# A layer kernel whose second token half is also given transposed: norms spread on chip, rows no longer turned, fold stores on ACT's queue

## The chip, the cores and the metric

The kernel runs on one core of one Trainium2 chip. The metric is the device time of one execution in microseconds; the time before is the median of three runs. A profiled execution was recorded besides; its page and its trace are quoted in the text. Engines are named as the profile names them: PE (TensorE matmul), PEld (its weight load), DVE (VectorE), ACT (ScalarE), POOL (GpSimd), SP (SyncE, which here issues most DMAs).

## What is computed

One layer of a streaming encoder on 2048 tokens of width 1024, all in fp32. It has three sub-layers, each between two RMS norms:

```python
u = rms_norm(h, g_mix_pre); z = u @ w_in          # 1024 -> 2816 columns
qa, ka, va, qh, fh, ih, gh = jnp.split(z, IN_SPLITS, axis=-1)
ya = swa_with_sinks(qa, ka, va, sinks)            # sliding-window attention
yh = hgrn2(qh, fh, ih, gh, lb, onorm)             # gated linear recurrence, log of fh
h = h + rms_norm(concat(ya, yh) @ w_out, g_mix_post)
h = h + rms_norm(cross_attention(rms_norm(h, g_x_pre), rms_norm(mem, g_mem), wq, wk, wv, wo), g_x_post)
h = h + rms_norm(swiglu(rms_norm(h, g_ffn_pre)), g_ffn_post)
```

The change touches the first norm and the first projection, `u @ w_in`, and one stage that prepares the cross-attention.

## The kernel before

**Matmuls.** Every fp32 operand is kept as two parts of a lower precision, hi and lo (`split`, `split2`: hi is a copy made on ACT or POOL, lo is the difference made on DVE), and a product is three matmuls: hi hi, hi lo, lo hi (`mm3`, and `products` at lines 1032 to 1034). Most large products are done in blocks of 2 x 2 by seven products in place of eight (`seven`; kind `"o"` here), the first two blocks of the first projection by eight (`eight`, kinds `"q"` and `"p"`). A step is one of these products: 12 matmuls of 128x128 by 128x512.

**First half of the first projection** (`in_first`, `in_block`). The tokens are cut in two halves of 1024. For the first half, rows of x are loaded, normed (`normed`: Square with a row sum on ACT, two small operations on POOL for the reciprocal root, a scaling on DVE), turned by TensorE (line 449) and kept in four tiles, `raw`. Eleven blocks of 256 columns of `w_in` then run in the order of `ORDER`. `phases` drives them: at each step it traces the step's matmuls, then the operands of the step two ahead (`upto(g + 2)`), then one piece of what a former block left to do (`after`), then pieces of the resident operands `T`. Within a step, line 1047 copies a bank of PSUM away on ACT (`part`), and `out` puts results into a `pair` tile.

**What runs beside.** While the blocks run, the eight rows tiles of the second token half are prepared: `stream` loads one into a `pair` tile (lines 542 to 545; `beside` says which block takes which), `after` norms it (572 and 573) and, some steps later, turns it with eight transposes on TensorE and two ACT copies (`transposed`, lines 1284 and 1285) and stores it to `un_d` in device memory (587). At the end `fetch` loads `un_d` back in four tiles of 1 MB (489), and lines 519 to 527 split these into the hi and lo parts `u` with which the second half is projected.

**Gate columns.** Four of the blocks (columns 1280 to 1791, `C_FH`) hold the forget gate. For these `after` runs `decays`: the logarithm (637, ACT, with a table load before and after), a scan on DVE, a shift on POOL and three exponentials on ACT, one piece a step.

**Later stages.** The second half is projected (`in_proj`, `in_cols`) beside attention (`swa`) and recurrence (`hgrn`). `fold_cross` multiplies the cross-attention's weights with the memory: it stores eight row tiles to `qk_d` (321) and eight to `vo_d` (347), at the end of that stage with nothing beside it. Then the remaining blocks run, again through `phases`; their left operands are streamed from `y_d`, which attention and recurrence wrote.

**Order.** The kernel names engines, tiles and buffers (a pool tag has a fixed number of buffers, `bufs`). The framework makes each engine's queue from that when the program is built (line 1662): an instruction may be placed ahead of others that were traced before it when its operands and its buffer are ready earlier. `behind` ties the instructions in it to come after the last ACT and DVE instruction traced up to `mark`. Each engine works off its queue in order; a DMA that waits on SP's queue holds up the DMAs behind it. All DMAs but those with accumulation are issued by SP (`load`, `store`).

Of the kernel before, what the change touches and what calls it, by code (L numbers as in the profile page):

```python
# [11 lines left out]
F32 = mybir.dt.float32  # L12
# [6 lines left out]
P = 128  # L19
# [29 lines left out]
class Layer:  # L49
# [27 lines left out]
    def store(self, dst, src):  # L77
        self.nc.sync.dma_start(dst, src)
# [13 lines left out]

    def rstd(self, parts, n, role):
# [9 lines left out]
        r = self.small(role + "_r")  # L103
        nc.gpsimd.tensor_tensor(r, v, self.mhalf[:, 0:1], ALU.pow)
        return r
# [62 lines left out]
    def run(self):  # L168
# [4 lines left out]
        self.y_d = tc.dram_tile([NT, P, KT, P], F32, name="y_d")  # L173
        self.un_d = tc.dram_tile([KT, P, TB], F32, name="un_d")
        self.h1t_d = tc.dram_tile([NT, P, KT, P], F32, name="h1t_d")
# [101 lines left out]
    def fold_cross(self):  # L277
# [31 lines left out]
        for d in range(KT):  # L309
            th, tl = self.wcols(self.I["wq_x"], d, "A")  # L310
            o = self.io_tile("x")
            for q in range(2):
# [7 lines left out]
                if q:  # L320
                    self.store(self.qk_d[d * P:(d + 1) * P, :], o)
                yield
        for vT in projected(self.I["wv_x"]):
            yield
        for h in range(4):
# [17 lines left out]
            for mt in range(2):  # L343
                o = self.io_tile("x")
                for q in range(2):
                    nc.scalar.activation(o[:, q * 512:(q + 1) * 512], banks[mt][q], AF.Copy)
                self.store(self.vo_d[(2 * h + mt) * P:(2 * h + mt + 1) * P, :], o)
            yield
# [73 lines left out]
    def in_first(self):  # L422
# [60 lines left out]
        second = {}  # L483

        def fetch():
            for s in range(2):
# [11 lines left out]
        phases = self.phases([(lambda i, j, a, n: raw[i, j][:, a:a + n, :], 4, blocks, None, {})], T)  # L498
        next(phases)
# [14 lines left out]
        for _ in phases:  # L514
            pass
        for _ in get:
            pass
        u = []
        for s in range(2):
            u.append([])  # L520
            for q in range(2):
                self._n += 1
                t = self.big.tile([P, 2, 4, 512], F32R, tag="big", name=f"u1_{q}{s}")
                r = second[q, s]
                for k in (0, 2):
                    self.split2(r[:, k:k + 2], t[:, 0, k:k + 2], t[:, 1, k:k + 2], "A")
                u[s] += [(t[:, 0, k, :], t[:, 1, k, :]) for k in range(4)]
        return u

    def in_block(self, ca, cb, beside, get, between):  # L530
# [405 lines left out]
    def combined(self, get, nk, dst):  # L936
# [3 lines left out]
        for a, b in halves:  # L940
            def put(key, t, o, op):
                with self.behind():
# [3 lines left out]
            for x, y, key in (((0, 1), (0, 0), 5), ((1, 1), (0, 1), 7), (None, (0, 0), 6), (None, (1, 0), 4)):  # L946
# [5 lines left out]
                if key == 4:  # L952
                    put(4, o, t, ALU.subtract)
                else:
                    put(key, t, o, ALU.add if key == 6 else ALU.subtract)
                yield
# [709 lines left out]
```

## Time and profile before

| | |
|---|---|
| median of 3 runs | 2603.19 us (2600.45 to 2605.1) |
| the profiled execution | 2603.6 us |
| its span, from first to last instruction | 2601.7 us |
| mean granted clock of TensorE | 0.992 |
| first projection, first half | from the start to about 263 us |
| fold | ends at about 791 us |

A row of the profile's groups reads: line, engine, operation, tile written <- tiles read, shape, count | busy us, mean ns of one | idle us of the engine just before them, and what ended most of it. A row of a timeline has the start, the duration, the engine, the line, and in brackets the idle time before it with what ended that. A row of waits has the total, the times and the longest. The chain of waits is followed back from the last instruction to what released each.

### The profile page before, as it was taken

To read this page: it belongs to the slowest core of one execution; us is meant where nothing else is said; L and a number is where in the kernel's file an instruction comes from. 1 tells how busy PE (TensorE), PEld (TensorE's weight loads), DVE (VectorE), ACT (ScalarE), POOL (GpSimd) and SP (SyncE) were. 2 spreads that over 40 slices of the span, in tenths; PEclk is the share of its full clock that TensorE was granted. 3 is DMA by queue.
4 is the path that set the end of the run, shared out by engine and by line. 5 is a ranking of instruction groups with operands and counts; after the bars stand their busy time and mean duration, and the time that the engine had idled before them with its cause. 6 is when DMAs were issued, how large, how long until landed. Compare 5 with 4: busy or idle time off the path is not lost.

```text
span 2601.7 us, 34516 instructions
## 1 busy us (share of the span) xinstructions
PE 2528.0 (97%) x12160; PEld 2115.2 (81%) x12160; DVE 1746.0 (67%) x2773; ACT 1262.0 (49%) x2641; POOL 466.6 (18%) x651
## 2 busy tenths in 40 slices
PE   7989999999998999999999999999999999999998
PEld 6878788878997778888778888888888888888786
DVE  7675578887646568786785555576666656664756
ACT  5463366655654565565563333354333335443543
POOL 4240343320312224223320000000000000000022
PEclk9999999999999999999999999999999999999999
DMA  5434655484875998656984532353456434576798
GB/s 186 143 120 167 208 157 171 131 267 157 279 259 207 289 328 258 221 191 187 302 273 138 167 124 73 105 186 116 167 182 230 147 108 168 174 225 174 232 228 208
DMA packets 286350, 497.88 MB, mean 191 GB/s; under 512 B 20576, under 2 KB 143456, under 8 KB 286176
## 3 DMA queue, kind: packets, MB, share of 16 engines
q1 hardware_dynamic: 275520, 456.87, 52.3%
q0 software_dynamic: 10656, 38.80, 8.0%
q8 instruction: 96, 1.57, 0.2%
q14 instruction: 78, 0.64, 0.1%
HBM read 328.87 MB, written 166.72 MB: 190 GB/s over the span
## 4 chain that ended last, share of the span: by engine, by line
PE 80%; DMA 8%; DVE 4%; issue 3%; POOL 2%; ACT 2%; SPq 0%; DVEq 0%; POOLq 0%; ACTq 0%
PE psm L1032 22%; PE psm L1034 22%; PE psm L1033 22%; PE psg L163 2%; PE psg L164 2%; PE psg L165 2%; DMA row<-in_x_dram 1%; PE pss L1284 1%; DMA row<-h_d 1%; DMA u_d<-row 1%; DMA h_d<-row 1%; DMA x<-in_w_out_dram 1%; ACT junk L1369 1%; DMA pair<-in_x_dram 1%; DMA extra<-qk_d 0%
## 5 line engine op out<-in xcount | busy, mean ns | idle before, releaser
L1032 PE MATMUL psm<-T,S 128*128 128x512 f32 x2664 | 1036.4, 393 | 24.6 <-ACT S L896 13.8
L1033 PE MATMUL psm<-T,S 128*128 128x512 f32 x2664 | 1041.9, 391 | 0.0
L1034 PE MATMUL psm<-T,S 128*128 128x512 f32 x2664 | 1037.3, 392 | 2.6 <-DVE S L899 2.5
L1032 PEld LDWEIGHTS psm<-T,S 128*128 128x128 f32 x2664 | 503.3, 189 | 132.6 <-ACT S L896 15.1
L1034 PEld LDWEIGHTS psm<-T,S 128*128 128x128 f32 x2664 | 502.5, 189 | 109.2 <-DVE S L899 4.8
L1033 PEld LDWEIGHTS psm<-T,S 128*128 128x128 f32 x2664 | 503.2, 189 | 103.3
L896 ACT ACTIVATE S<-sum 128x512 fp32r<-128x512 f32 (+1 forms) x338 | 208.0, 619 | 340.1 <-PE psm L1034 331.7
L899 DVE TENSOR_TENSOR S<-sraw,S 128x512 fp32r<-128x512 f32 (+1 forms) x311 | 214.4, 697 | 224.4 <-ACT S L896 214.9
L899 DVE TENSOR_TENSOR S<-sum,S 128x512 fp32r<-128x512 f32 (+1 forms) x404 | 277.1, 690 | 84.3 <-ACT S L896 66.6
L1047 ACT ACTIVATE part<-psm 128x512 f32<-128x512 f32 x297 | 175.1, 592 | 174.9 <-PE psm L1034 168.0
L896 ACT ACTIVATE S<-sraw 128x512 fp32r<-128x512 f32 (+1 forms) x272 | 166.8, 617 | 154.7 <-PE psm L1034 143.1
L1398 POOL DMA_DIRECT2D row<-y_d x28 | 25.0, 892 | 1131.4 <-DMA sraw<-hid_d 964.8
L1369 ACT ACTIVATE junk<-row 128x512 f32<-128x512 f32 x160 | 99.7, 624 | 121.8 <-DVE row L1391 33.4
L899 DVE TENSOR_TENSOR T<-row,T 128x1024 fp32r<-128x1024 f32 x104 | 123.0, 1190 | 28.7 <-ACT T L896 28.5
L163 PE MATMUL psg<-u,whi 128*128 128x512 f32 x352 | 141.2, 401 | 1.0 <-POOL whi L145 1.0
L165 PE MATMUL psg<-u,wlo 128*128 128x512 f32 x352 | 139.5, 396 | 1.5 <-DVE wlo L146 1.5
L164 PE MATMUL psg<-u,whi 128*128 128x512 f32 x352 | 139.6, 397 | 0.0
L896 ACT ACTIVATE T<-row 128x1024 fp32r<-128x1024 f32 x104 | 105.8, 1027 | 23.7 <-DMA row<-in_w_down_dram 10.9
L146 DVE TENSOR_TENSOR wlo<-raw,whi 128x1024 fp32r<-128x1024 f32 x54 | 68.8, 1275 | 33.2 <-ACT whi L143 26.6
L898 POOL TENSOR_SCALAR S<-sum 128x512 fp32r<-128x512 f32 x66 | 49.0, 742 | 234.7 <-PE psm L1034 141.0
L1550 DVE TENSOR_TENSOR part<-psm,part 128x512 f32<-128x512 f32 x66 | 45.4, 688 | 64.6 <-PE psm L1034 64.5
L1541 DVE TENSOR_TENSOR row<-psm,part 128x512 f32<-128x512 f32 x66 | 45.5, 689 | 57.4 <-PE psm L1034 57.3
(329 smaller groups left out, 3644.3 us busy)
## 6 DMA issues: line engine op xcount, KB each, us to landing
sraw<-in_w_gate_dram SPq DMA_DIRECT2D x44, 512.0 KB, 4.9
sraw<-in_w_up_dram SPq DMA_DIRECT2D x44, 512.0 KB, 4.8
hid_d<-row SPq DMA_DIRECT2D x44, 512.0 KB, 2.7
h_d<-row SPq DMA_DIRECT2D x32, 512.0 KB, 6.9
y_d<-row SPq DMA_DIRECT2D x32, 512.0 KB, 3.6
sraw<-hid_d SPq DMA_DIRECT2D x32, 512.0 KB, 5.2
row<-h_d POOLq DMA_DIRECT2D x30, 512.0 KB, 8.1
row<-y_d POOLq DMA_DIRECT2D x28, 512.0 KB, 7.3
```

The lines of the kernel that those rows point to most:

```text
L146: nc.vector.tensor_tensor(lo, raw, f32(hi), ALU.subtract)
L163: nc.tensor.matmul(ps, ah, bh, start=(i == 0), stop=False)
L164: nc.tensor.matmul(ps, ah, bl, start=False, stop=False)
L165: nc.tensor.matmul(ps, al, bh, start=False, stop=(i == n - 1))
L896: self.nc.scalar.activation(hi, raw, AF.Copy)
L898: self.nc.gpsimd.tensor_scalar(hi, raw, 1.0, 1.0, ALU.mult, ALU.mult)
L899: self.nc.vector.tensor_tensor(lo, raw, f32(hi), ALU.subtract)
L1032: nc.tensor.matmul(ps, s[:, 0, k, :], t[:, 0, k, :], start=st, stop=False, **kw)
L1033: nc.tensor.matmul(ps, s[:, 0, k, :], t[:, 1, k, :], start=False, stop=False, **kw)
L1034: nc.tensor.matmul(ps, s[:, 1, k, :], t[:, 0, k, :], start=False, stop=sp, **kw)
L1047: nc.scalar.activation(t, ps, AF.Copy)
L1369: self.nc.scalar.activation(junk, a, AF.Square, scale=float(D) ** -0.5, accum_out=to)
```

## The change

Five things, which belong together except for the last.

- The host also hands over the second token half of x transposed, as `x_t` in four tiles of 128 x 4 x 512, and the gain `g_mix_pre` with a column per 128 features, `g_mix_t`. `fetch` loads these instead of `un_d`, two tiles a block from the blocks after the seventh on; `un_d`, the transposes and the stores are gone.
- The rows of the second half are still loaded, but only for their sums of squares: into a tag `xr` with one buffer, Square in place, and the reciprocal root goes into a column of `r_u`. One row tile belongs to each of the blocks 1 to 8. `pair` has six buffers instead of five.
- Beside the last block (`{10: [scaled]}`), `scaled` spreads the eight columns of `r_u` along the partitions with eight transposes into two banks, and multiplies the loaded tiles by gain and norms, four DVE operations of 128 x 512 a step, in four steps. `parted` then splits as before.
- `decays` yields once more before the logarithm.
- The stores to `qk_d` and `vo_d` are issued from ACT's queue (`put`) instead of SP's.

```diff
+    def put(self, dst, src):
+        self.nc.scalar.dma_start(dst, src)
...
-                    self.store(self.qk_d[d * P:(d + 1) * P, :], o)
+                    self.put(self.qk_d[d * P:(d + 1) * P, :], o)
...
-                self.store(self.vo_d[(2 * h + mt) * P:(2 * h + mt + 1) * P, :], o)
+                self.put(self.vo_d[(2 * h + mt) * P:(2 * h + mt + 1) * P, :], o)
...
-        return self.st_pool.tile([P, 2, D], F32, tag="pair", name=f"pair_{self._n}", bufs=5)
+        return self.st_pool.tile([P, 2, D], F32, tag="pair", name=f"pair_{self._n}", bufs=6)
...
-                    self.load(r, self.un_d[4 * q:4 * q + 4, :, s * 512:(s + 1) * 512].rearrange("k p t -> p k t"))
+                    self.load(r, I["x_t"][2 * s + q])
...
+        def scaled():
+            banks = []
+            for s in range(2):
+                ps = self.bank("sh"[s])
+                for i in range(4):
+                    n = 4 * s + i
+                    nc.tensor.transpose(ps[:, i * P:(i + 1) * P], self.r_u[:, n:n + 1].broadcast_to([P, P]), self.ident)
+                banks.append(ps)
+            for s in range(2):
+                for q in range(2):
+                    r = second[q, s]
+                    for k in range(4):
+                        with self.behind():
+                            nc.vector.scalar_tensor_tensor(r[:, k, :], r[:, k, :], g_t[:, 4 * q + k:4 * q + k + 1],
+                                                           banks[s], ALU.mult, ALU.mult)
+                    yield
...
-        beside = [(), (0,), (1, 2), (3,), (4,), (5,), (6,), (7,), (), (), ()]
+        beside = [(), (0,), (1,), (2,), (3,), (4,), (5,), (6,), (7,), (), ()]
...
-                  + self.in_block(*p, beside[i], get if i > 9 else (), None if i else lambda: x_loads(0, (2, 3)))
+                  + self.in_block(*p, beside[i], get if i > 7 else (), None if i else lambda: x_loads(0, (2, 3)))
...
-            for n in beside:
-                t = self.pair_tile()
-                self.load(t[:, 0, :], self.I["x"][TB + n * P:TB + (n + 1) * P, :])
-                x.append((n, t))
-            for _ in range(3):
+            for _ in range(2):
                 next(iter(get), None)
...
         def after():
-            for n, p in x:
-                self.normed(p[:, 0, :], p[:, 1, :])
+            for n in beside:
+                self._n += 1
+                t = self.st_pool.tile([P, D], F32, tag="xr", name=f"xr_{self._n}", bufs=1)
+                self.load(t, self.I["x"][TB + n * P:TB + (n + 1) * P, :])
+                x.append((n, t))
...
-            for _ in range(1 if C_FH <= c0 < C_IH else 4):
+            for _ in range(1 if C_FH <= c0 < C_IH else 3):
                 yield
-            for n, p in x:
-                self.store_transposed(self.un_d, n, self.transposed(p[:, 0, :], p[:, 1, :]))
+            for n, t in x:
+                ss = self.small("n_s")
+                nc.scalar.activation(t, t, AF.Square, accum_out=ss)
+                self.rstd([ss], D, "n", self.r_u[:, n:n + 1])
                 yield
...
         NCB = TB // 64
+        yield
         nc.scalar.activation(e1, f, AF.Ln)
```

More of the change, by code (lines that the diff above doesn't have):

```diff
@@ L91, in gain, with rstd @@
         return g
-    def rstd(self, parts, n, role):
+    def rstd(self, parts, n, role, r=None):
         nc = self.nc
@@ L102, in rstd @@
             nc.gpsimd.tensor_scalar(v, parts[0], 1.0 / n, EPS, ALU.mult, ALU.add)
-        r = self.small(role + "_r")
+        if r is None:
+            r = self.small(role + "_r")
         nc.gpsimd.tensor_tensor(r, v, self.mhalf[:, 0:1], ALU.pow)
@@ L173, in run @@
         self.y_d = tc.dram_tile([NT, P, KT, P], F32, name="y_d")
-        self.un_d = tc.dram_tile([KT, P, TB], F32, name="un_d")
         self.h1t_d = tc.dram_tile([NT, P, KT, P], F32, name="h1t_d")
@@ L483, in in_first @@
         second = {}
+        self.r_u = self.mc.tile([P, NPB], F32, name="r_u")
+        g_t = self.mc.tile([P, KT], F32, name="g_t")
+        u = [[], []]
         def fetch():
+            self.load(g_t, I["g_mix_t"])
             for s in range(2):
@@ L488, in fetch, with parted @@
                     r = self.pair_tile().rearrange("p a d -> p (a d)").rearrange("p (k t) -> p k t", k=4)
-                    self.load(r, self.un_d[4 * q:4 * q + 4, :, s * 512:(s + 1) * 512].rearrange("k p t -> p k t"))
+                    self.load(r, I["x_t"][2 * s + q])
                     second[q, s] = r
                     yield
-        beside = [(), (0,), (1, 2), (3,), (4,), (5,), (6,), (7,), (), (), ()]
+        def scaled():
[14 more added lines that the diff above has]
+                    yield
+        def parted():
+            for s in range(2):
+                for q in range(2):
+                    self._n += 1
+                    t = self.big.tile([P, 2, 4, 512], F32R, tag="big", name=f"u1_{q}{s}")
+                    for k in (0, 2):
+                        self.split2(second[q, s][:, k:k + 2], t[:, 0, k:k + 2], t[:, 1, k:k + 2], "A")
+                    u[s] += [(t[:, 0, k, :], t[:, 1, k, :]) for k in range(4)]
+        beside = [(), (0,), (1,), (2,), (3,), (4,), (5,), (6,), (7,), (), ()]
         get = fetch()
         blocks = [("q" if i == 0 else "p" if i < 2 else "o",)
-                  + self.in_block(*p, beside[i], get if i > 9 else (), None if i else lambda: x_loads(0, (2, 3)))
+                  + self.in_block(*p, beside[i], get if i > 7 else (), None if i else lambda: x_loads(0, (2, 3)))
                   for i, p in enumerate(self.ORDER)]
-        phases = self.phases([(lambda i, j, a, n: raw[i, j][:, a:a + n, :], 4, blocks, None, {})], T)
+        phases = self.phases([(lambda i, j, a, n: raw[i, j][:, a:a + n, :], 4, blocks, None, {10: [scaled]})], T)
         next(phases)
@@ L515, in in_first @@
             pass
[L516 to L527, printed above, removed]
+        parted()
         return u
@@ L571, in after @@
         def after():
-            for n, p in x:
-                self.normed(p[:, 0, :], p[:, 1, :])
+            for n in beside:
+                self._n += 1
+                t = self.st_pool.tile([P, D], F32, tag="xr", name=f"xr_{self._n}", bufs=1)
+                self.load(t, self.I["x"][TB + n * P:TB + (n + 1) * P, :])
+                x.append((n, t))
             c0 = ca * P
@@ L940, in combined, with made @@
         for a, b in halves:
-            def put(key, t, o, op):
+            def made(key, t, o, op):
                 with self.behind():
@@ L952, in combined @@
                 if key == 4:
-                    put(4, o, t, ALU.subtract)
+                    made(4, o, t, ALU.subtract)
                 else:
-                    put(key, t, o, ALU.add if key == 6 else ALU.subtract)
+                    made(key, t, o, ALU.add if key == 6 else ALU.subtract)
                 yield
@@ L1657 @@
             host[name] = tiled(host[name].T if name == "wq_x" else host[name])
+    host["x_t"] = np.ascontiguousarray(host["x"][TB:].reshape(2, 512, 2, 4, P).transpose(0, 2, 4, 3, 1)).reshape(4, P, 4, 512)
+    host["g_mix_t"] = np.ascontiguousarray(host["g_mix_pre"].reshape(KT, P).T)
     nc = _bacc.Bacc("TRN2", target_bir_lowering=False, num_devices=1, dynamic_dma_scratch_size=2048)
```

## The prediction

> **What bounds the kernel now.** First the page, for the engine that sets the end.
>
> ```profile
> span 2601.7 us, 34516 instructions
> ...
> PE 2528.0 (97%) x12160; PEld 2115.2 (81%) x12160; DVE 1746.0 (67%) x2773; ACT 1262.0 (49%) x2641; POOL 466.6 (18%) x651
> ```
>
> TensorE is busy for 97% of the span. So a microsecond comes off the end only where TensorE gets less work or waits less; work taken from another engine counts only where TensorE waits for it. Second, busy time in stretches (length, then PE, PEld, DVE, ACT and POOL busy with counts, granted clock, DMA share, GB/s).
>
> ```profile
> 0.00:40.00 40.00, 25.72 (x170) 23.16 (x171) 26.42 (x37) 25.31 (x47) 22.01 (x39) 1.00 0.56 197
> 40.00:100.00 60.00, 60.00 (x270) 49.73 (x269) 46.31 (x53) 26.17 (x41) 11.05 (x17) 1.00 0.44 149
> ...
> 138.00:171.00 33.00, 27.02 (x114) 21.87 (x112) 25.75 (x31) 20.01 (x31) 15.99 (x18) 0.90 0.38 124
> ...
> 243.00:275.00 32.00, 27.81 (x119) 21.56 (x118) 23.70 (x27) 13.03 (x18) 13.17 (x12) 1.00 0.65 223
> ...
> 700.00:790.00 90.00, 88.65 (x659) 84.00 (x658) 42.18 (x54) 51.95 (x115) 19.39 (x23) 1.00 0.77 261
> 790.00:802.00 12.00, 5.06 (x15) 3.67 (x14) 2.63 (x4) 3.22 (x6) 0.47 (x1) 0.72 0.89 298
> ```
>
> The change touches four leaky places: the start, the gate-column blocks (138 to 171, with the clock at 0.90), the passage into the second half's projection (243 to 275), and the passage from the fold to the mixed blocks (790 to 802, clock 0.72). Third, what TensorE waits for between 100 and 200, and ACT's timeline there.
>
> ```profile
> PE psm L1032 <- ACT part L1047: 6.2, 3, 3.9
> ```
>
> ```profile
> 132.23 1.06 ACT L418 ACTIVATE pair<-pair 128x1024 f32<-128x1024 f32 x1 [4.32 <-DMA pair<-in_x_dram]
> ...
> 140.41 0.59 ACT L1047 ACTIVATE part<-psm 128x512 f32<-128x512 f32 x1
> ...
> 157.48 1.06 ACT L418 ACTIVATE pair<-pair 128x1024 f32<-128x1024 f32 x1 [3.41 <-DMA pair<-in_x_dram]
> ```
>
> ACT stands 4.32 and 3.41 us in the Square of a second-half row whose load has not landed. The bank copy `part` that TensorE needs is queued behind, with the logarithm and its table loads.
>
> **The change, part by part.**
>
> *Transposes.* Of the eight turned rows, one in the chain of waits and all of them by line:
>
> ```profile
> 206.34 0.87 PE pss L1284 x8
> ```
>
> ```profile
> L1284 PE MATMUL pss<-ident,pair x64: 270/272/328, 37.3 to 206.9; 128*128 128x128 f32 x64
> ```
>
> Eight transposes take 0.87 us of TensorE. 64 leave and 8 of the same shape come (the norms, spread): 7 x 0.87 = **-6.1 us**, on the path with certainty.
>
> *The Square's wait.* A row now has a buffer of its own (one), not one of the five `pair` buffers. Loads here go out as soon as their buffer is free, however early that is: the gain that only the fold uses, a stage far behind, is loaded the moment the last norm of x has released its buffer.
>
> ```profile
> 161.63 0.33 SPq L75 DMA_DIRECT2D g<-in_g_mem_dram  x1
> ```
>
> So I expect the eight rows to chase each other (load, Square, next load) from the start on, and all Squares to be over before 132 us, where the first harmful one stood. Then the 6.2 us of `part` waits go, and with them the slow matmuls after each: 8 and 5 at 0.43 where 0.23 is normal.
>
> ```profile
> 142.49 0.43 PE psm L1034
> ...
> 145.47 0.42 PE psm L1032
> 145.90 0.23 PE psm L1033
> ```
>
> ```profile
> 167.62 0.43 PE psm L1033
> ...
> 169.33 0.43 PE psm L1034
> ```
>
> 13 x 0.20 = 2.6, with 6.2 together 8.8. Bounds: 0 (something else holds `part`) and -8.8. I take **-8.0**, nearly all, since in both places the wait for the row is the longest that ACT has before the copy. The logarithm one step later is priced at nothing: its place in ACT's queue follows its input, POOL's product.
>
> *What the Squares cost at the start.* They meet a queue that is short there (engines' share in tenths over 0 to 30 us; then size and median time to landing; ACT's waits up to 270 us):
>
> ```profile
> DMA  0059999999999999999999999999999300000000
> ...
> x<-in_x_dram SPq DMA_DIRECT2D x8, 512.0 KB, 8.0
> ```
>
> ```profile
> pair<-in_x_dram SPq DMA_DIRECT2D x8, 512.0 KB, 5.8
> ```
>
> ```profile
> ACT pair L418 <- DMA pair<-in_x_dram: 15.0, 5, 4.3
> ```
>
> DMA is full until 24 us, so the first Squares may wait, 3.0 us each by the waits row; from 24 to 30 it is idle, and between 40 and 100 TensorE never stopped although a wait as long lay there:
>
> ```profile
> 60.09 1.07 ACT L418 ACTIVATE pair<-pair 128x1024 f32<-128x1024 f32 x1 [3.95 <-DMA pair<-in_x_dram]
> ```
>
> From below, no cost; from above, all eight waits passed on, 24 us. I take one, **+3.0**, being nearest to the full stretch of 40 to 100.
>
> *Scaling.* Sixteen DVE products of 128x512 with PSUM as an operand, all behind the last group's first four steps, replace eight of 128x1024 that were spread. Nearest row for one, then DVE's groups from 238 to 274 (busy, mean | idle before), and the first wait at the passage:
>
> ```profile
> 248.03 0.69 DVE L569 SCALAR_TENSOR_TENSOR pair<-th,psm 128x512 f32<-128x512 f32 x1 [1.39 <-ACT th L568]
> ```
>
> ```profile
> L899 DVE TENSOR_TENSOR u<-pair,u 128x1024 fp32r<-128x1024 f32 x8 | 10.6, 1356 | 0.6 <-ACT u L896 0.6
> ...
> L556 DVE TENSOR_TENSOR pair<-psm,part 128x512 f32<-128x512 f32 x5 | 3.3, 687 | 6.9 <-issue 4.7 <-PE psm L1034 2.2
> ...
> L569 DVE SCALAR_TENSOR_TENSOR pair<-th,psm 128x512 f32<-128x512 f32 x2 | 1.4, 680 | 1.4 <-ACT th L568 1.4
> ```
>
> ```profile
> PE psg L165 <- DVE wlo L146: 1.5, 1, 1.5
> ```
>
> ```profile
> 265.20 1.21 DVE L146 TENSOR_TENSOR wlo<-raw,whi 128x1024 fp32r<-128x1024 f32 x1
> ```
>
> 16 x 0.69 = 11.0 us of DVE against 6.9 + 1.4 = 8.3 us of idle: 2.7 us too much. Queued behind are the `u` low parts and `wlo`, for whose first piece TensorE already waits at the passage. So **+2.7**; bounds 0 (the products start a group earlier, or the passage hangs on something else) and +11.0 (no cover).
>
> *Cheap parts.* 16 ACT copies of turned rows and 4 MB of `un_d` stores go, and neither is among TensorE's waits above. The four 1 MB loads stay, from `x_t`, with no store to wait for; they hold four of six `pair` buffers from the seventh block on, leaving two for results, which are stored within a block: nothing. Past SP's queue nothing else moves; POOL keeps its two norm operations per row.
>
> *Fold stores.* SP's, ACT's and TensorE's timelines at the passage, and the chain behind it:
>
> ```profile
> 758.29 0.33 SPq L78 DMA_DIRECT2D y_d<-sg  x1
> ```
>
> ```profile
> 779.36 11.33 SPq L78 DMA_DIRECT2D vo_d<-x  x5
> 790.78 1.25 SPq L75 DMA_DIRECT2D sraw<-y_d  x2
> ```
>
> ```profile
> 790.71 0.62 ACT L346 ACTIVATE x<-psh 128x512 f32<-128x512 f32 x1
> 796.82 0.63 ACT L896 ACTIVATE S<-sraw 128x512 fp32r<-128x512 f32 x1 [5.50 <-DMA sraw<-y_d]
> ```
>
> ```profile
> 797.50 0.79 PE L1032 MATMUL psm<-T,S 128*128 128x512 f32 x1 [6.94 <-ACT S L896]
> ```
>
> ```profile
> 798.30 0.43 PE psm L1033
> ...
> 800.86 0.41 PE psm L1033
> ```
>
> SP sits 11 us behind stores that wait for ACT's copies; only then do the next stage's loads leave. Their rows were written by 758 us, and their buffers lie where the finished recurrence's were. On ACT's queue the stores hold up no load: data are there by 790, and TensorE starts after ACT's last copy (791.33), two issues of 0.33, a split of 0.63 and 0.05 of signal, at 792.7 instead of 797.5: **-4.8**. Bounds: 0, if the loads' buffers come free only at 790, and -8.3, if the whole wait of 6.9 and the seven slow matmuls behind it (7 x 0.20) go. The slow ones stay in my sum, as an idle of 2.2 us was enough for the eight at 142.
>
> ACT's own price, its issues, by SP's row for such a store:
>
> ```profile
> L78 SPq DMA_DIRECT2D vo_d<-x x8: 319/326/464, 771.7 to 792.1; - x8
> ```
>
> 16 x 0.33 = 5.2 us beside ACT's 52 of 90 busy: hidden, 0; uncovered +5.2. Queued behind a store on ACT are the weight splits.
>
> [...]
>
> [...] As a variant of the forecast it has a tenth of its chance: 2589.0.
>
> **Sum.** -6.1 - 8.0 + 3.0 + 2.7 - 4.8 = -13.2. From the profiled execution's 2603.6 (its span and 1.9 around it) that is 2590.4; it lies 0.4 above the median of 2603.19, which I take to come out the same: **2590.4 us**.
>
> **Rivals.**
> 1. *The waits only move.* The Squares stall TensorE as much at the start as they did in the gate blocks. For it: the same 5.8 us landings. Against it: 60.00 of 60. The 8.0 are not won: 2598.4.
> 2. *The fold part gives nothing* (the loads' buffers come free only with the last copies): 2595.2. [...]
> 3. *Slower: one row buffer makes a chain on ACT.* Eight Squares in a row, each in ACT's queue ahead of splits and copies, each waiting 3.0 us for a load that cannot leave before the previous Square. It decides once ACT's waits outrun the two steps by which operands are made ahead, 24 x 0.23 = 5.5 us, that is from the second full wait in a row on. Priced with all of them passed on, +24.0 for +3.0: 2611.4. Against it: DMA is idle from 24 us on, where most of the chain should lie.
> 4. *DVE has no cover at the passage*: TensorE stands for all of the new products, +11.0 for +2.7: 2598.7. For it: `wlo` is waited for already. Against it: DVE's 8.3 us of idle.
>
> **Chances.** Forecast 0.50; rival 1 0.15; rival 2 0.14; rival 3 0.15; rival 4 0.06. Range: below, every unknown at its good end, -6.1 - 8.8 - 8.3 = 2580.4; above, through rivals 1 and 4 with another 6 us of the first Squares' waits, 2605; left out is rival 3, and a little at the low end. A measurement of this kernel tells about 0.2%, 5.2 us, from no change: faster is below 2598.0. Forecast and rival 2 lie there, rivals 1 and 4 on the edge, counted a third: 0.70. Same 0.14, slower 0.16.
>
> **What would show it.** Right: 64 transposes gone from the rows of `pair`, 8 new ones; Squares of the second half's rows before 132 us; no `part` wait over 1 us between 100 and 200 and the clock at 1.00; `sraw<-y_d` issued before 785, TensorE's wait at the passage near 2 us instead of 6.94. Wrong: PE short of 40 in the stretch 40 to 100, or a longer start, with ACT waiting for rows (rivals 1, 3); TensorE waiting for DVE's new products or for `wlo` by more than 3 us (rival 4); or new transposes that wait for a norm, which I priced at nothing.

## The result: 2607.32 us, a little slower than before

The changed kernel takes 2607.32 us (median of 20 runs, 2604.86 to 2612.01); the kernel before, measured again beside it, 2603.9 us (20 runs, 2599.03 to 2609.62). The ratio is 1.0013, with a 95% interval of 1.0007 to 1.0019: 3.4 us slower, within the 0.2% that I had called no change, and 17 us above the forecast of 2590.4 and outside its range, which ended at 2605. The profiled execution took 2606.15 us.

First the page of the changed kernel, the two lines that were read first for the kernel before.

```profile
span 2604.4 us, 34334 instructions
...
PE 2532.0 (97%) x12104; PEld 2108.2 (81%) x12104; DVE 1735.2 (67%) x2781; ACT 1256.3 (48%) x2625; POOL 461.2 (18%) x651
```

The transposes are gone (12104 matmuls where 12160 were), and yet TensorE is busy for 4.0 us longer, in a span that is 2.7 us longer. In sum, its loss is not idle time. The same stretches as before say where (length, then PE, PEld, DVE, ACT, POOL busy with counts, granted clock, DMA share, GB/s):

```profile
40.00:100.00 60.00, 59.62 (x251) 47.64 (x252) 40.47 (x49) 23.29 (x36) 15.70 (x19) 0.96 0.36 123
138.00:171.00 33.00, 31.57 (x135) 24.93 (x134) 24.92 (x36) 19.81 (x31) 13.25 (x19) 1.00 0.27 98
243.00:275.00 32.00, 25.64 (x100) 20.06 (x99) 24.34 (x28) 11.20 (x15) 11.22 (x11) 0.89 0.53 177
...
790.00:802.00 12.00, 8.86 (x29) 6.27 (x30) 3.94 (x6) 5.79 (x10) 0.73 (x1) 0.86 0.79 285
```

The gate blocks (138 to 171) and the passage after the fold (790 to 802) went the way of the forecast: 31.57 busy for 27.02 and clock 1.00 for 0.90 in the first, 8.86 busy for 5.06 in the second. The passage at 243 got worse, 25.64 for 27.81. The row 40 to 100 is one to stop at: TensorE is almost as busy as before, with 251 matmuls in it where 270 were. The clock (0.96 in the row, 0.55 from 40 to 45 us and 1.00 after that) accounts for a part of that only.

Set the two traces against each other matmul by matmul (the n-th of the 9736 with 512 columns, in each), and the delay of the changed kernel grows and shrinks like this. The numbers are differences of start times, stretch by stretch, in us; the rows below the first are experiments that come later. "Best version" is the fastest kernel of experiments 10 to 12.

| stretch of before | 0 to 65 | 65 to 193 | 193 to 281 | 281 to 642 | 642 to 799 | 799 to 1300 | 1300 to 1383 | 1383 to end | sum |
|---|---|---|---|---|---|---|---|---|---|
| changed kernel | +4.2 | -10.5 | +5.4 | +4.4 | -2.3 | -0.6 | +2.5 | -0.4 | +2.7 |
| changed, shifted to 512 bytes | +3.9 | -12.6 | +5.1 | +2.2 | -2.6 | +1.6 | +2.7 | -0.1 | +0.1 |
| that, fold stores on SP | +3.1 | -12.6 | +4.7 | +1.7 | +1.0 | -0.9 | +2.7 | +1.0 | +0.7 |
| before, shifted by 64 bytes | +0.9 | +0.9 | +2.1 | +2.9 | +0.1 | -0.8 | +0.9 | +0.1 | +7.0 |
| before, fold stores on ACT | +0.1 | -0.4 | +0.4 | +1.3 | -6.7 | -2.0 | +0.5 | -0.5 | -7.3 |
| best version | +4.3 | -12.6 | -3.9 | +8.8 | -5.6 | +1.8 | +1.8 | -0.8 | -6.3 |

Three cautions belong to this table. Each row is one profiled execution, and such an execution can lie 6 us off the median of its kernel (2596.11 against 2602.12 with the fold stores on ACT); from 799 to 1300 us, where all these kernels run the same instructions, the rows still differ by -2.0 to +1.8. The edge at 193 us stands just ahead of a wait of 1.7 us, for DVE's low part of an operand `S`, which the changed kernel shifted to 512 bytes has and the kernel before has not: up to 200 us its -12.6 is -10.6. The edge at 281 us stands just ahead of the best version's longest wait, so that a loss of the passage is counted in its next column: from 237 to 295 us the changed kernel shifted to 512 bytes loses 4.9 us and the best version 1.6, from 295 to 642 us 1.2 and 2.6.

**What the forecast had right.** The Squares of the second half's rows run early, from 24 to 58 us, with short waits for their loads; the gate blocks wait 0.7 us at most for `part`; eight short transposes are left; and the fold's next loads are issued at 781 instead of 791. From the timeline and the waits of ACT over 0 to 66 us, the waits of TensorE from 100 to 200, the instructions of line 507 and SP's timeline:

```profile
24.23 1.11 ACT L610 ACTIVATE xr<-xr 128x1024 f32<-128x1024 f32 x1
...
56.69 1.06 ACT L610 ACTIVATE xr<-xr 128x1024 f32<-128x1024 f32 x1 [1.63 <-DMA xr<-in_x_dram]
```

```profile
ACT xr L610 <- DMA xr<-in_x_dram: 7.6, 6, 2.5
```

```profile
PE psm L1057 <- ACT part L1072: 2.6, 4, 0.7
```

```profile
L507 PE MATMUL pss<-ident,r_u x8: 271/347/475, 40.3 to 82.5; 128*128 128x128 f32 x8
```

```profile
781.03 19.15 SPq L75 DMA_DIRECT2D sraw<-y_d  x6
```

**What it had wrong.** Most of what I said would prove the steps is there, and the time did not fall. Two things spent it. One is the pace. Here are ten matmuls in a row of the kernel before and ten of the changed one, first and last (TensorE's timeline: start, duration, line):

```profile
75.18 0.39 PE L1033 MATMUL psm<-T,S 128*128 128x512 f32 x1
...
77.22 0.39 PE L1033 MATMUL psm<-T,S 128*128 128x512 f32 x1
```

```profile
75.26 0.39 PE L1057 MATMUL psm<-u,S 128*128 128x512 f32 x1
...
77.36 0.39 PE L1057 MATMUL psm<-u,S 128*128 128x512 f32 x1
```

Nine steps take 2.04 us before and 2.10 us after, 227 and 233 ns each, with nothing waiting and the clock at 1.00. This distance from one start to the next, where nothing waits, is called the pace here. Up to 660 us, 478 of 1816 such steps take 229 ns or more in the kernel before, and 1614 of 1822 in the changed one. What the steps take beyond 226.7 ns (2.04 us over nine) adds up to 2.8 us before and 10.7 after: **7.9 us** that no view of waits shows, because nobody waits.

The other is the passage. TensorE's longest wait there, and DVE's timeline ahead of it:

```profile
PE psm L1057 <- DVE pair L575: 4.7, 1, 4.7
```

```profile
257.27 0.68 DVE L588 SCALAR_TENSOR_TENSOR pair<-th,pair 128x512 f32<-128x512 f32 x1
257.87 2.71 DVE L514 SCALAR_TENSOR_TENSOR pair<-pair,g_t,pss 128x512 f32<-128x512 f32 x4
260.51 0.68 DVE L575 TENSOR_TENSOR pair<-psm,part 128x512 f32<-128x512 f32 x1
```

Four of the new products stand ahead of the sum that frees TensorE's bank, and ten matmuls at 0.43 us follow the wait. A shorter wait, 1.6 us for DVE's low part of `S`, stands at 245 us already, with two of the new products ahead of it in DVE's queue.

### The profile page after: what moved, and what is told of

Read it like the earlier page. It is cut to its first block, busy times and chain, and to the rows that moved or that the text cites. A ratio compares the mean times of both kernels' runs of the same rounds, so it can differ in the third digit from the quotient of the medians.

```text
span 2604.4 us, 34334 instructions
## 1 busy us (share of the span) xinstructions
PE 2532.0 (97%) x12104; PEld 2108.2 (81%) x12104; DVE 1735.2 (67%) x2781; ACT 1256.3 (48%) x2625; POOL 461.2 (18%) x651
## 4 chain that ended last, share of the span: by engine, by line
PE 81%; DMA 7%; DVE 5%; issue 3%; ACT 2%; POOL 2%; SPq 0%; DVEq 0%; POOLq 0%; ACTq 0%
PE psm L1057 22%; PE psm L1059 21%; PE psm L1058 21%; PE psg L168 2%; PE psg L167 2%; PE psg L169 2%; PE pss L1309 1%; DMA u_d<-row 1%; DMA row<-in_x_dram 1%; DMA sraw<-in_w_in_dram 1%; DMA row<-h_d 1%; DVE S L924 1%; DMA row<-qk_d 1%; DMA extra<-qk_d 0%; ACT junk L1394 0%
## 5 line engine op out<-in xcount | busy, mean ns | idle before, releaser
L1057 PE MATMUL psm<-T,S 128*128 128x512 f32 x2664 | 1035.1, 393 | 22.4 <-ACT S L921 10.7
```

Of the source, the lines that this page charges most:

```text
L1057: nc.tensor.matmul(ps, s[:, 0, k, :], t[:, 0, k, :], start=st, stop=False, **kw)
```

## The experiments

All ratios are to the kernel before, run beside on the same chip. "Shifted" means that one tile that nothing reads or writes is laid into the pool `mc`; the pool `big`, with the operand tiles `u0`, `u1` and some of the `T`, lies ahead of `mc`, the pools with `S`, the other `T` and the split weights behind it. The change itself put two tiles there: `r_u` and `g_t`, eight columns of 4 bytes each, 64 bytes together.

### 1 to 5: is the pace a matter of place?

Theory P: the 64 bytes changed where left and right operand of a matmul lie to each other, and that sets the pace. Rival W: the pace comes with the change's traffic, and the waits ate the gain.

The changed kernel with 64 bytes more, 128 in all:

```diff
         g_t = self.mc.tile([P, KT], F32, name="g_t")
+        self.mc.tile([P, 16], F32, name="shift")
```

> The changed kernel with one unused tile of 64 bytes per partition more, laid behind r_u and g_t, so that every tile behind them lies 128 bytes higher than in the kernel before, where the change had them 64 bytes higher. Theory P (pace): from 65 to 650 us TensorE's matmuls follow each other at 233 ns in the changed kernel and at 227 ns in the kernel before, in some 1460 matmuls, because left and right operand no longer lie alike in 128 bytes. It expects 227 ns again and 1460 x 6.6 ns = 9.6 us less: 2597.7 us, a ratio of 0.9976 to the kernel before, and the rest of the trace as in the changed kernel. Rival W (waits): the slower pace comes from something that the change does (its loads, more DVE traffic) and what ate the gain are the waits at the start, at the passage and in the fold; then the 64 bytes change nothing, 2607 us, 1.0013.

Measured 1.0007 (0.9997 to 1.0018), 2608.83 us. The pace came back only in part: 1503 of 1817 steps still took 229 ns or more. As stated, the theory's number was a miss; either the theory is wrong or 128 bytes are not the right distance.

The kernel before with 64 bytes, and with 32 (`[P, 8]`):

```diff
         second = {}
+        self.mc.tile([P, 16], F32, name="shift")
```

> The kernel before with nothing but one unused tile of 64 bytes per partition at the place where the change puts r_u and g_t. No instruction differs. Theory P: 1460 matmuls at 233 ns where they took 227: +9.6 us, 2613.5 us, a ratio of 1.0037. Rival W: the same time as the kernel before, 2603.9 us.

> The kernel before with an unused tile of 32 bytes per partition at the same place. If, by theory P, any difference of place within 128 bytes costs the 6.6 ns, the time is as with 64 bytes, 2613.5 us; if only whole steps of 64 bytes count, 2603.9 us; a part of it if the cost grows with the distance. By rival W nothing changes.

Measured 1.0025 (1.0016 to 1.0033) with 64 bytes, 2610.86 us; 1.0012 (1.0003 to 1.0021) with 32, 2609.7 us. No instruction was added. Ten steps of the kernel with 64 bytes, at the same place of its trace:

```profile
84.18 0.39 PE L1034 MATMUL psm<-u,S 128*128 128x512 f32 x1
...
86.28 0.39 PE L1034 MATMUL psm<-u,S 128*128 128x512 f32 x1
```

2.10 us for nine steps, as in the changed kernel, and 1621 of 1816 at 229 ns or more. Rival W cannot explain this: an unused tile of 64 bytes makes a kernel 6.5 us slower (4.2 to 8.6). With 32 bytes as many steps are long (1598 of 1819), yet the time rose by 3.1 us only (0.8 to 5.5), less than the 7.4 us that its steps add up to; why stays open.

The kernel before with 256 bytes (`[P, 64]`), and the changed kernel with 448, that is 512 in all (`[P, 112]`):

> The kernel before with an unused tile of 256 bytes per partition where the change puts r_u and g_t; the question is the pace between 70 and 120 us. If the period of the place is 256 bytes, matmuls follow each other at 227 ns as in the kernel before; if it is 512 bytes, slower, as with 128 bytes (230 to 233 ns).

> The changed kernel with an unused tile of 448 bytes per partition behind r_u and g_t, so that everything behind lies 512 bytes higher than in the kernel before. The run with 128 bytes in all kept a pace of 230 to 233 ns where before has 227, so 128 bytes are not the period that counts. In the kernel before, all those operands lie a multiple of 512 bytes apart. Theory P2: the period is 512 bytes (or a part of it that 128 is not a multiple of); 227 ns comes back, 1460 x 6.6 = 9.6 us less than the changed kernel: 2597.7 us, a ratio near 0.9975. Rival (any shift of these tiles costs the same, whatever its size): 2607 to 2609 us, 1.001.

Measured 0.9992 (0.9982 to 1.0002) with 256 bytes, 2603.95 us, and 0.9985 (0.9975 to 0.9995) for the changed kernel with 512, 2602.37 us. First and last of ten steps of either:

```profile
83.88 0.39 PE L1035 MATMUL psm<-u,S 128*128 128x512 f32 x1
...
85.92 0.39 PE L1035 MATMUL psm<-u,S 128*128 128x512 f32 x1
```

```profile
84.12 0.39 PE L1058 MATMUL psm<-T,S 128*128 128x512 f32 x1
...
86.16 0.39 PE L1058 MATMUL psm<-u,S 128*128 128x512 f32 x1
```

2.04 us again: 227 ns, with 465 and 451 slow steps. So a period of 256 bytes fits all the places that were tried (192 and 384 bytes were not), 128 is not enough, and the changed kernel at such a place is 0.28% faster than as it was given, about 7.3 us by 0.0028 x 2605 (the intervals of the two ratios leave some 4 to 10), against 7.9 us counted from its trace. This is the largest single part of the miss.

### 6 and 7: the fold stores alone, and with a fourth buffer

The kernel before with nothing but `put` in the two places of the diff, and then with `bufs=4` instead of 3 for the stored row tiles:

> The kernel before with the fold's stores issued from ACT's queue and nothing else. The prediction gave this -4.8 us: 2599.1. From the changed kernel's trace, where a copy on ACT waits 4.9 us for a store of vo_d to land while the next stage's loads run, I now expect less, -1 to -2.5 us: 2601.4 to 2602.9. Rival: the wait is only exchanged, 2603.9 or up to 1 us more.

> The kernel before with the fold's stores on ACT's queue and four buffers instead of three for the stored row tiles. The stores alone gave -4.4 us, with ACT's copy waiting 2.5 us for a store to land, which did not reach TensorE there. Theory: the fourth buffer then adds nothing that can be measured here, -4 to -5 us, 0.998. Rival: copies that leave sooner pull the end of the fold forward as well: -6 us or more, 0.9975.

Measured 0.9983 (0.9972 to 0.9994), 2602.12 us, and 0.9983 (0.9973 to 0.9993), 2601.18 us: -4.4 us in both (-7.3 to -1.6 and -7.0 to -1.8). Waits of TensorE and of ACT from 780 to 802 in the first:

```profile
PE psm L1035 <- ACT S L899: 1.8, 1, 1.8
```

```profile
ACT x L349 <- DMA vo_d<-x: 2.5, 1, 2.5
```

TensorE's wait is 1.8 where the kernel before had 6.94. ACT does wait for a store to land, but TensorE has enough ahead, so the fourth buffer is worth nothing here. My second thought, that the part would bring only 1 to 2.5 us, did not come true, though the ends of the intervals touch it.

### 8: the transposed half alone

The changed kernel at 512 bytes with the fold stores back on SP (`store` for `put`):

> The run with 448 bytes and the fold's stores back on SP's queue: the transposed half alone, at the pace of before. The prediction gave this part -6.1 - 8.0 + 3.0 + 2.7 = -8.4 us. Theory: from the trace of the run with 448 bytes (start +3.9, 64 to 193 us -12.6, then +5.1 to 281 and +2.2 to 642 us), -1.4 us by 642 us, and with the stores on SP no gain in the fold: 0 to +2 us, a ratio near 1.0000 to 1.0005. Rival: the fold part is what fails inside the changed kernel and the transposed half brings what was forecast, -5 us or more: 0.998.

Measured 1.0006 (0.9997 to 1.0016), 2607.61 us. At the old pace the transposed half, for which the forecast had -8.4 us, changes the time by +1.6 us (-0.8 to +4.2): it wins nothing. With the stores on ACT the same kernel is at 0.9985, so they are worth about 5.5 us inside the change. TensorE's wait at the fold's end is the old one:

```profile
PE psm L1058 <- ACT S L922: 7.2, 1, 7.2
```

### 9: the scaling a block earlier

```diff
-                    yield
+                        if k % 2:
+                            yield
...
-        beside = [(), (0,), (1,), (2,), (3,), (4,), (5,), (6,), (7,), (), ()]
+        beside = [(0,), (1,), (2,), (3,), (4,), (5,), (6,), (7,), (), (), ()]
...
-        phases = self.phases([(lambda i, j, a, n: raw[i, j][:, a:a + n, :], 4, blocks, None, {10: [scaled]})], T)
+        phases = self.phases([(lambda i, j, a, n: raw[i, j][:, a:a + n, :], 4, blocks, None, {9: [scaled]})], T)
```

> The run with 448 bytes, and the scaling one block earlier: scaled runs beside block 9 instead of 10, two products a step instead of four, and each row of the second half one block earlier. Theory: in the changed kernel TensorE stands 4.9 us at the passage, because four products of 2.71 us stand in DVE's queue ahead of the sum that frees its bank, and ten slow matmuls of 2.0 us follow; with two products a step these go: 5 to 7 us less than the run with 448 bytes alone. Rival: DVE has as much to do there, and the wait shows up at another sum: less than 1.5 us.

Measured 0.9984 (0.9974 to 0.9994), 2600.53 us: as the run with 512 bytes alone. The wait for DVE is gone, and one of 6.4 us stands a few microseconds later (TensorE's waits from 237 to 285, then ACT's timeline):

```profile
PE psg L167 <- ACT z L639: 6.4, 1, 6.4
```

```profile
270.43 0.63 ACT L703 ACTIVATE qs<-qd 128x512 fp32r<-128x512 f32 x1 [14.33 <-DMA qd<-z_d]
270.96 0.58 ACT L639 ACTIVATE z<-psg 128x512 f32<-128x512 f32 x1
```

ACT stands 14.33 us in the first copy for attention, whose load of `z` is issued at 266.65 us; the copy of a projected column, whose matmuls were over by 265.2 us, is queued behind it. The rival was right in that the wait shows up elsewhere and nothing is gained, but not in the place: it is no other sum of DVE's, it is ACT's copy.

### 10 to 12: what holds the passage then

The scaling early and four buffers in the fold; then also three column blocks of the projection ahead of attention instead of two; then, in place of that, the attention copy tied behind the first two column copies:

```diff
+            if len(cols) == 2 and not s:
+                self.mark()
...
-            nc.scalar.activation(q, qd, AF.Copy, scale=-0.125)
+            with self.behind() if n == 0 else contextlib.nullcontext():
+                nc.scalar.activation(q, qd, AF.Copy, scale=-0.125)
```

> The changed kernel with 448 bytes, the scaling a block earlier, and four buffers for the stored row tiles, with the Squares left at the start. In the run without the fourth buffer TensorE stood 1.9 us in the fold for a copy that waited 4.8 us for a store. Theory: with the fourth buffer that wait and the slow matmuls behind it go (1.9 + 1.4): 3 us less than that run, a ratio of 0.997. Rival: the next stage's loads then land later and take its place: 0.9984 as before.

> The same with one column block more of the second half's projection ahead of the first attention block. With the scaling early, TensorE came to the passage 6 us sooner and stood 6.5 us there, because ACT's copy of a projected column stood behind the first attention copy, which waited 14.3 us for its load of z. Theory: the third column block's copies go ahead of that, TensorE has 5.5 us more work of its own, and the wait goes: 4 to 6 us less than the run without it, near 0.995. Rival: attention starts later and ends its stage later, so the time comes back between 280 and 650 us: no change.

> The run with 448 bytes, early scaling and four buffers, and the first attention copy of q tied behind the first two copies of projected columns on ACT. In the run without it ACT has the attention copy first, waiting for its load of z until 270.4 us, and TensorE stands 6.9 us at 266 us for the copy of a projected column behind it. Theory: the order of these two on ACT is what holds the passage once the scaling is early; the 6.9 us go and 4 to 6 us reach the end: 0.996. Rival: attention, started later, then ends its stage later, as with the third column block: 0.998 to 1.000.

Measured 0.9979 (0.9969 to 0.9989), 2600.09 us; 0.9998 (0.9987 to 1.0009), 2603.43 us; and **0.9965 (0.9952 to 0.9978), 2596.62 us**, the fastest kernel of the study, 9.1 us below the kernel before. The third column block did not go ahead of the attention copy, so the wait stayed and only the drawback came: its trace loses 5.7 us between 642 and 799 us, where the run without it wins 4.4. TensorE's longest wait from 237 to 285 us in the three:

```profile
PE psg L167 <- ACT z L639: 6.8, 1, 6.8
```

```profile
PE psg L167 <- ACT z L639: 7.0, 1, 7.0
```

```profile
PE psg L167 <- ACT z L639: 4.4, 1, 4.4
```

and ACT's timeline in the last, with the column copies now ahead:

```profile
261.20 0.60 ACT L639 ACTIVATE z<-psg 128x512 f32<-128x512 f32 x1 [3.91 <-PE psg L169]
266.64 0.60 ACT L639 ACTIVATE z<-psg 128x512 f32<-128x512 f32 x1 [4.84 <-PE psg L169]
273.31 0.63 ACT L706 ACTIVATE qs<-qd 128x512 fp32r<-128x512 f32 x1 [6.07 <-DMA qd<-z_d]
```

The order on ACT was one limit of the passage; the wait did not go but shrank, now behind a second attention copy that waits 6.64 us for its load, until 280.58 us. Most of the +8.8 that the table has from 281 to 642 us is no loss of the later stage: 6.1 of it is this wait and the slow matmuls behind it. From 237 to 295 us the passage costs 1.6 us where the kernel without the tie has 4.8, and from 295 to 642 us the two lose alike (2.6 and 2.8). So the traces speak for the theory, with about 3 us of its 4 to 6; they do not show attention ending later for it, as the rival had it. The two measured ratios (0.9965 and 0.9979) have intervals that overlap.

### 13 to 15: the Squares, and three repairs at once

Every Square tied to its block; then, with that, scaling early and four buffers; then, in the best version, only the first Square tied, so that the chain runs from 65 us on:

```diff
-                nc.scalar.activation(t, t, AF.Square, accum_out=ss)
+                with self.behind():
+                    nc.scalar.activation(t, t, AF.Square, accum_out=ss)
...
+                with contextlib.nullcontext() if n else self.behind():
```

> The run with 448 bytes, and each Square of a second-half row tied behind the ACT work traced up to its block, so that it stays in its block instead of running at the start. Theory: the eight Squares cost the start about 3.5 us (the first product 2.3 us later and another 1.2 by 65 us, beside the slower pace); this comes back, and in their blocks they cost nothing, as each row was loaded a block ahead: 2 to 3.5 us less than the run with 448 bytes alone. Rival: at the start it is the loads of the rows that delay, not the Squares, or the Squares delay copies in the gate blocks again: 0 or slower.

> The run with 448 bytes with three repairs at once: scaling a block earlier, Squares in their blocks, and four buffers instead of three for the row tiles that the fold stores (ACT stood 4.9 us there for a store to land). If each of them gives what was expected for it alone, with 2 to 3 us for the fourth buffer: 2597.7 - 6 - 2.8 - 2.5 = 2586 us, a ratio near 0.993. Rival: the repairs share one wait, 2592 us.

> The same with the first of the eight Squares tied to its block, so that the chain of row loads and Squares starts at 65 us instead of 20 and ends at about 100, ahead of the gate blocks. Theory: the Squares cost 4 us where they are, at the start, and nothing between 65 and 100 us, where TensorE never stops: 3 to 4 us less than the run without it. Rival: as with all Squares tied to their blocks, the wait only moves into the blocks: 0 or slower.

Measured 1.0007 (0.9997 to 1.0016), 2607.88 us; 0.9986 (0.9977 to 0.9995), 2601.18 us; 1.0003 (0.9993 to 1.0013), 2606.71 us. All three are misses. The start does come back: by 65 us the first is 0.5 us ahead of the kernel before and the third 1.3 behind, where the kernels of the table with 512 bytes are 3.1 to 4.3 behind. But the gate blocks then lose more. TensorE's waits from 100 to 192 us, in the first and in the third:

```profile
PE psm L1059 <- ACT part L1074: 5.2, 4, 1.8
PE pss L508 <- POOL r_u L108: 2.1, 3, 0.8
```

```profile
PE psm L1065 <- DVE S L930: 5.6, 3, 2.3
PE psm L1063 <- ACT S L927: 5.0, 2, 2.8
```

In the first, `part` waits again, and the spread transposes wait for their norms. The tied Square stands right ahead of the copy there: it runs from 135.54 us, the copy starts at 136.58, and TensorE waits 1.76 us for it. In the third the last Square is over at 103 us; one wait of 2.8 us is beside it, the other four, 7.8 us for split operands, come from 141 us on, with no Square near. Moving the Squares seems to have re-ordered what ACT and DVE do there. So what is won between 65 and 193 us hangs on the order of these queues as a whole, and the absence of the Square is not enough; which part of the order matters, the runs do not show. The third piece of the change there, the logarithm one step later, was in all of these kernels and was not tried alone.

### 16: the place in device memory

The best version with `un_d` declared again, unused, so that the tensors declared after it should have their old addresses:

```diff
         self.y_d = tc.dram_tile([NT, P, KT, P], F32, name="y_d")
+        tc.dram_tile([KT, P, TB], F32, name="un_d")
```

> The run with the attention copy tied behind, with the 4 MB tensor un_d declared again but neither written nor read, so that the tensors behind it in device memory (h1, u_s, hid and others) lie at the addresses of the kernel before. In the profiles of kernels with the transposed half, the stretch from 1300 to 1383 us, whose instructions do not differ, is 1.7 to 4.5 us longer than before, in nearly all of them, and not in those without it; TensorE waits there once more, for DVE's part of an operand. Theory: as with the tiles on the chip, the place in device memory makes these loads later; with the old places 2 to 3 us come back, 0.9955. Rival: the place in device memory does nothing: 0.9965 as without it, and the stretch stays longer.

Measured 0.9967 (0.9956 to 0.9978), 2596.82 us, and the stretch from 1300 to 1383 stays 2.6 us longer. Declaring it changes nothing, so the place in device memory is not the reason; why that stretch is longer stays open.

## Why the prediction was wrong, step by step

- **Cheap parts, 0.** This is the step that failed most. It went through loads, stores, copies and buffers, and left out where tiles lie. `r_u` and `g_t` move everything behind them by 64 bytes, which costs 7.9 us by the trace and about 7.3 by experiments 1 to 5. Neither the sum nor the range had a term for it. Nothing in the waits of the kernel before could have told this. The kernel's text had a hint, two tiles named `pad` that nothing reads, which I passed over.
- **Transposes, -6.1, and the Square's wait, -8.0.** Right in sign, and the Square did hold `part`, though by a way that the prediction did not name. The chain of waits of the kernel before goes from the landing of the row over the Square, POOL's norm operation and POOL's product ahead of the logarithm to the copy; the prediction had taken that product for the logarithm's own matter:

```profile
149.81 7.58 DMA pair<-in_x_dram
...
157.48 0.18 ACT pair L418
...
158.99 0.88 POOL n_r L104
...
160.53 2.76 POOL pair L564
...
166.28 0.50 ACT part L1047
```

  In the changed kernel `part` waits 2.6 us in all for 6.2, and no slow clock is left there. Between 65 and 193 us the kernel at the old pace wins 12.6 us; the wait of 1.7 us for `S` right behind the edge takes some of it back, and the transposes at 206 us add 0.9, so that by 237 us 11.5 of the 14.1 are won. The rest is in this wait, in `part` waits that stayed, four of up to 0.7, and in eight transposes that lay ahead of 65 us. Experiment 15 shows that the reason was too simple: Squares that are over before the blocks do not by themselves do it.
- **Squares at the start, +3.0.** About right: +3.1 to +4.3 by 65 us (0.9 of the given kernel's +4.2 is the pace), back to +1.3 or -0.5 where the Squares run later. That the number fits is in part luck. It was one wait of a Square passed on; in the trace TensorE waits 2.8 us for bank copies that stand behind Squares on ACT, where it waited 0.4 before, and the clock is 0.55 from 40 to 45 us, for which the term had nothing. (The sign "PE short of 40" in the stretch 40 to 100 is a slip: the stretch is 60 us long, and 59.62 of it are busy.)
- **Scaling, +2.7.** Too small, and for a wrong reason. The sum of DVE's idle time against new work is not what decides: the price of a product was right (2.71 us for four), but TensorE stood 4.7 us for one sum with four products queued ahead of it. From 193 to 281 us the loss is 4.7 to 5.4, and from 237 to 295, at the old pace, 4.9. The 1.7 to 2.2 that follow by 642 us cannot be put down to the scaling: the kernel before with the fold stores alone loses 1.3 there. Rival 4 named DVE, and its sign, a wait of more than 3 us for the new products, is there, but its price was wrong. Experiment 9 shows that DVE was not the only limit: once DVE was cleared, the same time was lost to ACT.
- **Fold stores, -4.8.** Right: -4.4 alone, about -5.5 inside. In the kernel before, five stores take 11.33 us on SP's queue, though the median issue of such a store is 0.33 us, and the next stage's loads behind them leave at 790.78 us; with the stores on ACT's queue they leave at 777.82 in experiment 6 and at 781.03 in the changed kernel. In the changed kernel a second wait came that I had not seen, 2.0 us inside the fold, where ACT's copy stood for a store to land (ACT's timeline from 776, TensorE's waits from 780 to 802):

```profile
790.62 0.60 ACT L349 ACTIVATE x<-pss 128x512 f32<-128x512 f32 x1 [4.89 <-DMA vo_d<-x]
```

```profile
PE pss L341 <- ACT x L349: 2.0, 1, 2.0
PE psm L1057 <- ACT S L921: 1.9, 1, 1.9
```

  The variant of the forecast at 2589.0 us leaves out the seven slow matmuls behind the passage (7 x 0.20 = 1.4). After the wait of 1.9 us there the changed kernel has none, but after the 2.0 us inside the fold it has seven.

- **The sum.** -13.2 was forecast. With the pace (7.3) it is -5.9, with some 2 us more at the passage near -4; the given kernel came out at +3.4. The remaining 7 us are spread, and single traces tell them only roughly: 2.6 between 65 and 237 us, some 2 in the fold, and 2.5 between 1300 and 1383, a stretch that is 1.8 to 4.7 us longer in the profiles of the kernels with the transposed half (0.7 in one of them) and -0.2 to 1.1 in those without it. That last part was not settled. Rivals 1 and 3 did not happen: the start cost little more than I had taken. The upper end of the range, 2605, had taken rivals 1 and 4 one at a time; both together are 2606.7 by the prediction's own terms.

## What to carry to other kernels

A new tile is not free because it is small (the 64 bytes of `r_u` and `g_t` cost about 7 us here): before adding one, look at what lies behind it, and where operands of a matmul lie in different pools, move the later pool by multiples of 256 bytes only, as far as the places tried here tell (256 and 512 bytes kept the 2.04 us for nine steps, 64 made it 2.10); the sign to look for is the same busy time of TensorE with fewer matmuls in it at a clock of 1.00 (from 45 to 100 us TensorE is busy for 55.00 us in both kernels, with 236 matmuls of 128x512 in the changed one and 240 before), or a longer way from the start of one matmul to the next. Do not compare an engine's idle time with new work to price a stage; look at which instruction TensorE needs next and what stands ahead of it in that queue. And when a wait is cleared, look at the next in line before counting the gain: here the wait of 4.7 us for DVE gave way to one of 6.4 us for ACT.

## What the runs showed of the hardware

- **The pace changed with the place.** With a shift of 0, 256 or 512 bytes between the pools nine steps take 2.04 us; with 32 or 64 bytes 2.10; with 128, 1503 of 1817 steps take 229 ns or more. Whether it is the place of the two operands to each other or each one's own was not separated, nor what in the chip does it.
- **The clock after short waits.** After the 2.0 us at 791 us in the changed kernel, seven matmuls follow at 0.42 us or more, with a granted clock of 0.50 from 792.5 to 795 us (two of them below, from TensorE's timeline, four steps and 1.71 us apart); after the 1.9 us at 799, and after the 1.8 us of experiment 6, none does. The eight at 142 us in the kernel before are less clear a case than the prediction made them: the wait is 2.04 us by the timeline, and eight transposes stand ahead of it, so that no other matmul runs for 2.9 us.

```profile
792.81 0.63 PE L341 MATMUL psh<-whi,kv 128*128 128x512 f32 x1
...
794.52 0.63 PE L343 MATMUL psh<-whi,kv 128*128 128x512 f32 x1
```
